# Second MLP: the weight sum for product N7 is tied to a place behind the remainder of the unit ahead

## The chip, the cores and the metric

The kernel runs on one core of one Trainium2 chip. The metric is device time in microseconds, from launch to end. Three runs of the kernel before gave 2282.0, 2282.33 and 2283.88 us, median 2282.33. The execution that was profiled took 2283.91 us itself, and its span from the first to the last instruction was 2282.1 us, so 1.81 us lie around the span.

## The reference

256 tokens of width 2048 go through one attention layer (MLA), a squared-ReLU MLP, one Mamba-2 layer and a second squared-ReLU MLP, all with RMS norm before and a residual sum behind. Only the second MLP is touched here. It is

```
h = rms_norm(x, mlp_norm_g[1])        # 256 x 2048
u = relu(h @ w_in)                    # w_in  2048 x 8192
x = x + (u * u) @ w_out               # w_out 8192 x 2048
```

in float32.

## The kernel before

**Exact products from halves.** A weight tile arrives in float32. ScalarE copies it to a rounded type (the high half, tile `wh`, L102), VectorE subtracts this from the original (the remainder, tile `wl`, L103), and TensorE forms three products: high by high (L619), high of the activations by remainder of the weights (L620), remainder of the activations by high (L621). So each weight tile of 128 x 1024 costs one ScalarE and one VectorE instruction before TensorE may read it. Such a tile is a *unit*. Units are numbered through the program and stand in one list; `wh819` and `wl819` are the two halves of unit 819. There are four buffers each for `wh` and `wl`, so the halves of unit 819 reuse those of unit 815 once TensorE is through with them. Six raw buffers hold tiles that come from memory, on SyncE's queue, in the order of the list.

**Seven products instead of eight.** The first matrix product of the MLP, with `w_in`, goes pair of column blocks by pair of column blocks: `p` counts the pairs, 0 to 7. Pair 0 is done plainly. For pairs 1 to 7, called passes here, the 2x2 blocks (two halves of the tokens, two halves of the input rows, two column blocks) are combined in the manner of Strassen, and the seven products have names: M1, N7, N5, N6, N4, M2, N3. Each comes in four units, `d` = 0 to 3, called quarters of the rows here. The weights of a quarter are b11, b12, b21 and b22. M1 takes b11 as it is. N7 needs b12 + b22, which VectorE adds in the place of b22 (L183). N5 then needs b11 + b12, added in the place of b12. N6 needs b11 + b12 + b22, added in the place of b11. M2, N3 and N4 need no sum on VectorE; N4's is made by a DMA of GpSimd that adds b21 onto the tile that N6 used. So N7's sum reads two tiles fresh from memory, while the other two sums read tiles that are there by then.

**The order of the list.** `plan()` interleaves the units of a pass with those of the second matrix product (`o`, with `w_out`, of the hidden blocks of earlier passes), by a table of costs. Units of a pass take 6 matmuls on TensorE, `o` units and the plain `c` units 12. Stretches of the list in the second MLP that are spoken of below:

| units | what they are |
|---|---|
| 695 to 702 | pass 1: M1, N7, N5, N6 of quarter 2; M1, N7, N5 of quarter 3; N4 of quarter 1 |
| 816, 817, 819, 820 | pass 4, quarter 0: M1, N7, N5, N6 (818 and 821 are `o` units) |
| 822, 823 | pass 4, quarter 1: M1, N7 |
| 829, 830, 831, 832, 833, 834 | pass 4: N6 of quarter 1; M1, N7 of quarter 2; an `o` unit, the last of its block; N5, N6 of quarter 2 |

**Who sets the order of the instructions.** TensorE's order is the order in which the program is written. On the other engines a scheduler sets it when the program is built, from its own estimates of when each instruction could run; each engine then takes its instructions strictly in that order, and one that waits holds back all behind it. `issue_after(ins)` is a tie: what is written under it may not stand ahead of `ins` on the engine of `ins`. `flow.last_lo` is the latest remainder that was written (the last L103), which is the one of the unit ahead in the list. The kernel before uses this tie for N7's sum in the Mamba-2 layer (`prefix == ("s",)`), not in the two MLPs (`prefix == ("s", 0)` and `("s", 1)`).

**Other work on the two engines.** VectorE also adds finished `o` blocks onto the residual (L438, two instructions, one for each half of the tokens), combines finished products (L623, L624) and makes remainders of hidden activations (L301). ScalarE also copies M1's finished product out of its bank (L633), applies ReLU and square (L579, L627, L569) and makes high halves of activations (L300).

Of the kernel before, what the change touches and what calls it, by code (L numbers as in the profile page):

```python
# [71 lines left out]
class Flow:  # L72
# [22 lines left out]
    def halves(self, raw, n, step=None):  # L95

        nc = self.nc
        h = self.pools["wh"].tile([P, 1024], F32R, tag="wh", name=f"wh{self.done}")
        lo = self.pools["wl"].tile([P, 1024], F32R, tag="wl", name=f"wl{self.done}")
        for o in range(0, n, step or n):  # L100
            v = slice(o, o + (step or n))
            self.last = nc.scalar.activation(h[:, v], raw[:, v], AF.Copy)  # L102
            self.last_lo = nc.vector.tensor_tensor(lo[:, v], raw[:, v], h[:, v].bitcast(F32), ALU.subtract)  # L103
        return h, lo
# [65 lines left out]
def seven(prefix, p, src):  # L170

    state = {}

    def quarter(d, i, j):
        return src[2 * i + d // 2, 2 * p + j][:, (d % 2) * 1024:(d % 2) * 1024 + 1024]

    def unit(flow, name, d):  # L180
        nc = flow.nc
        st = state.setdefault(d, {})
        add = lambda out, a, b: nc.vector.tensor_tensor(st[out].tile, st[a].tile, st[b].tile, ALU.add)  # L183
        halves = lambda q: flow.halves(st[q].tile, 1024)

        def make():
            if name == "N7":
                with flow.tc.issue_after(flow.last_lo.ins) if prefix == ("s",) else nullcontext():
                    add("b22", "b12", "b22")
                out = halves("b22")  # L190
                if d in LATE5:
                    nc.gpsimd.dma_start(st["b12"].tile, quarter(d, 0, 0), accum_op=ALU.add)
                return out
            if name == "N5" and d not in LATE5:
                add("b12", "b11", "b12")
                return halves("b12")
            if name == "N6":
                add("b11", "b11", "b22")
                out = halves("b11")
                nc.gpsimd.dma_start(st["b11"].tile, quarter(d, 1, 0), accum_op=ALU.add)  # L200
                return out
            return halves({"M1": "b11", "N4": "b11", "N5": "b12"}.get(name, name))

        def load(k, pool, q):
            st[k] = Load(pool, quarter(d, *q))
            return st[k]

        loads = {"M1": lambda: [load("b11", "rx", (0, 0))],
                 "N7": lambda: [load("b12", B12, (0, 1)), load("b22", "raw", (1, 1))],
                 "M2": lambda: [load("M2", "raw", (1, 0))], "N3": lambda: [load("N3", "raw", (1, 1))]}  # L210
        return Unit(prefix + (p, name, d), 2, 512, loads.get(name, list)(), make)

    return unit
# [1596 lines left out]
```

## Time and profile before

| what | us |
|---|---|
| profiled execution, own time | 2283.91 |
| its span | 2282.1 |
| TensorE busy in the span | 2269.3 (99%) |
| VectorE busy | 1965.0 (86%) |
| ScalarE busy | 1442.3 (63%) |
| second MLP, 1590 to 2282 us of the span | 692 |
| TensorE busy in it | 686.54 |
| VectorE busy in it | 604.76 |
| ScalarE busy in it | 422.84 |

The page of the profile lists for each engine its busy time, for each line of the program the time of its instructions, and for each wait the engine that ended it. TensorE is the engine that is nearly always busy. Its matmuls are pipelined: one of 512 columns is shown with some 0.39 us, but the next starts 0.23 us after it. So lost time on TensorE is best read from the starts of matmuls that follow each other: what goes beyond 0.23 us was lost. In rows of the timeline, the first number is the start in us from the start of the span, the second the duration; behind them stand engine, line, operation, tiles (out<-in) and count, and in brackets the idle time ahead of it and what ended it.

### The profile page before, as it was taken

To read this page: it belongs to the slowest core of one execution; us is meant where nothing else is said; L and a number is where in the kernel's file an instruction comes from. 1 tells how busy PE (TensorE), PEld (TensorE's weight loads), DVE (VectorE), ACT (ScalarE), POOL (GpSimd) and SP (SyncE) were. 2 spreads that over 40 slices of the span, in tenths; PEclk is the share of its full clock that TensorE was granted. 3 is DMA by queue.
4 is the path that set the end of the run, shared out by engine and by line. 5 is a ranking of instruction groups with operands and counts; after the bars stand their busy time and mean duration, and the time that the engine had idled before them with its cause. 6 is when DMAs were issued, how large, how long until landed. Compare 5 with 4: busy or idle time off the path is not lost.

```text
span 2282.1 us, 30858 instructions
## 1 busy us (share of the span) xinstructions
PE 2269.3 (99%) x10881; PEld 1880.4 (82%) x10881; DVE 1965.0 (86%) x2257; ACT 1442.3 (63%) x2044; POOL 284.9 (12%) x339
## 2 busy tenths in 40 slices
PE   9999999999999999999999999999999999999999
PEld 7898888888888888888888788888888888888887
DVE  7786697998998897879979998976989889989985
ACT  6775475666666666566677676565666665665663
POOL 1440000000000000100003532230000000000000
PEclk9999999999999999999999999999999999999999
DMA  8545778888888877768898888866788888888874
GB/s 316 173 153 156 214 229 263 261 258 267 264 254 259 270 236 245 237 190 272 262 368 284 290 290 310 295 220 218 215 256 253 254 270 251 262 275 238 264 233 162
DMA packets 176026, 569.74 MB, mean 250 GB/s; under 512 B 20192, under 2 KB 29344, under 8 KB 175872
## 3 DMA queue, kind: packets, MB, share of 16 engines
q1 hardware_dynamic: 147808, 498.24, 65.2%
q0 software_dynamic: 16320, 56.88, 11.9%
q10 hardware_dynamic: 11744, 12.66, 1.8%
q8 instruction: 85, 1.39, 0.2%
q14 instruction: 69, 0.57, 0.1%
HBM read 542.23 MB, written 6.41 MB: 240 GB/s over the span
## 4 chain that ended last, share of the span: by engine, by line
PE 93%; DVE 3%; DMA 2%; ACT 1%; issue 1%; POOL 0%; SPq 0%; ACTq 0%; DVEq 0%
PE acc L340 10%; PE acc L341 10%; PE acc L344 10%; PE yp L621 9%; PE yp L620 9%; PE yp L619 9%; PE st L620 7%; PE st L621 7%; PE st L619 7%; DVE wl L103 1%; DMA wraw<-mi 1%; PE st L1164 1%; PE st L1162 1%; PE st L1163 1%; PE yp L340 1%; PE yp L341 1%
## 5 line engine op out<-in xcount | busy, mean ns | idle before, releaser
L102 ACT ACTIVATE wh<-wraw 128x1024 fp32r<-128x1024 f32 (+1 forms) x818 | 857.3, 1053 | 531.2 <-PE acc L341 179.8
L103 DVE TENSOR_TENSOR wl<-wraw,wh 128x1024 fp32r<-128x1024 f32 (+1 forms) x818 | 988.2, 1227 | 179.0 <-ACT wh L102 168.9
L619 PE MATMUL yp<-wh,k 128*128 128x512 f32 x896 | 349.3, 390 | 0.0
L621 PE MATMUL yp<-wh,k 128*128 128x512 f32 x896 | 348.8, 389 | 0.0
L620 PE MATMUL yp<-wl,k 128*128 128x512 f32 x896 | 348.6, 389 | 0.0
L102 ACT ACTIVATE wh<-wrx 128x1024 fp32r<-128x1024 f32 x192 | 203.2, 1059 | 168.7 <-PE yp L621 99.6
L103 DVE TENSOR_TENSOR wl<-wrx,wh 128x1024 fp32r<-128x1024 f32 x192 | 233.6, 1222 | 41.0 <-ACT wh L102 39.5
L340 PE MATMUL acc<-wh,k 128*128 128x512 f32 x496 | 196.9, 397 | 0.3 <-ACT k L300 0.3
L621 PEld LDWEIGHTS yp<-wh,k 128*128 128x128 f32 x896 | 168.2, 188 | 35.1
L619 PEld LDWEIGHTS yp<-wh,k 128*128 128x128 f32 x896 | 168.3, 188 | 34.8
L620 PEld LDWEIGHTS yp<-wl,k 128*128 128x128 f32 x896 | 168.2, 188 | 34.8
L341 PE MATMUL acc<-wh,k 128*128 128x512 f32 x496 | 193.7, 391 | 0.6 <-DVE k L301 0.6
L340 PE MATMUL acc<-wh,xt 128*128 128x512 f32 x480 | 191.6, 399 | 0.9 <-ACT wh L102 0.9
L341 PE MATMUL acc<-wh,xt 128*128 128x512 f32 x480 | 187.4, 390 | 0.2 <-DVE xt L484 0.2
L619 PE MATMUL st<-wh,xt 128*128 128x512 f32 x448 | 177.7, 397 | 0.0
L621 PE MATMUL st<-wh,xt 128*128 128x512 f32 x448 | 174.9, 390 | 0.0
L620 PE MATMUL st<-wl,xt 128*128 128x512 f32 x448 | 174.7, 390 | 0.0
L200 POOL DMA_DIRECT2D wrx<-mi x56 | 49.0, 875 | 723.8 <-DVE wl L103 513.0
L620 PE MATMUL st<-wl,sN 128*128 128x512 f32 x336 | 131.5, 391 | 2.9 <-DVE wl L103 2.9
L619 PE MATMUL st<-wh,sN 128*128 128x512 f32 x336 | 133.3, 397 | 0.1
L344 PE MATMUL acc<-wl,k 128*128 128x512 f32 x496 | 132.7, 389 | 0.0
L621 PE MATMUL st<-wh,sN 128*128 128x512 f32 x336 | 131.1, 390 | 0.0
(342 smaller groups left out, 3808.2 us busy)
## 6 DMA issues: line engine op xcount, KB each, us to landing
wraw<-mi SPq DMA_DIRECT2D x256, 512.0 KB, 5.7
wraw<-mo SPq DMA_DIRECT2D x256, 512.0 KB, 5.3
wraw<-si SPq DMA_DIRECT2D x160, 512.0 KB, 6.1
wraw<-so SPq DMA_DIRECT2D x64, 512.0 KB, 5.1
wrx<-mi SPq DMA_DIRECT2D x56, 512.0 KB, 5.4
wrx<-mi POOLq DMA_DIRECT2D x56, 512.0 KB, 7.7
wraw<-wo SPq DMA_DIRECT2D x32, 512.0 KB, 3.8
tap<-xD SPq DMA_DIRECT2D x24, 512.0 KB, 8.2
```

What stands on the lines that cost most here:

```text
L102: self.last = nc.scalar.activation(h[:, v], raw[:, v], AF.Copy)
L103: self.last_lo = nc.vector.tensor_tensor(lo[:, v], raw[:, v], h[:, v].bitcast(F32), ALU.subtract)
L200: nc.gpsimd.dma_start(st["b11"].tile, quarter(d, 1, 0), accum_op=ALU.add)
L340: nc.tensor.matmul(accs[t][:, :n], ah, wh[:, q, :], start=first and kt + q == 0, stop=False)
L341: nc.tensor.matmul(accs[t][:, :n], al, wh[:, q, :], start=False, stop=False)
L344: nc.tensor.matmul(accs[t][:, :n], lhs(kt + q, t)[0], wl[:, q, :], start=False, stop=en and q == nk - 1)
L619: nc.tensor.matmul(b, ah, wh, start=first and q == 0, stop=False)
L620: nc.tensor.matmul(b, ah, wl, start=False, stop=False)
L621: nc.tensor.matmul(b, al, wh, start=False, stop=last and q == 1)
L1162: nc.tensor.matmul(bank[onto], ah, wh, start=done + q == 0 and not skip, stop=False, skip_group_check=skip)
L1163: nc.tensor.matmul(bank[onto], al, wh, start=False, stop=False, skip_group_check=skip)
L1164: nc.tensor.matmul(bank[onto], ah, wl, start=False, stop=done == 3 and q == 1, skip_group_check=skip)
```

## The change

In the second MLP, N7's sum (L183 under `if name == "N7"`) is now tied behind the latest remainder, in all passes and quarters but pass 1, quarter 0: 27 of its 28 sums. The first MLP stays as it was, and the Mamba-2 layer too.

```
-                with flow.tc.issue_after(flow.last_lo.ins) if prefix == ("s",) else nullcontext():
+                with flow.tc.issue_after(flow.last_lo.ins) if prefix == ("s",) or prefix == ("s", 1) and (p, d) != (1, 0) else nullcontext():
                     add("b22", "b12", "b22")
```

No instruction is added or taken away. The orders of TensorE, GpSimd and SyncE's queue are the same; VectorE's and ScalarE's differ from the second MLP's pass 1 on. Three places:

VectorE in pass 4, quarters 0 and 1 (`wl819`, `wl820`: remainders of N5 and N6 of quarter 0; `wraw823_17479`: the sum for N7 of quarter 1; `wrx816`: the sum for N6 of quarter 0):

```order
-L183 TENSOR_TENSOR wraw823_17479<-wraw823_17477,wraw823_17479 128x1024
+L183 TENSOR_TENSOR wrx816_17365<-wrx816_17365,wraw817_17379 128x1024
 L301 TENSOR_TENSOR k4_1173_17317<-sm_1181_17455,k4_1172_17316 128x4x128
 L103 TENSOR_TENSOR wl819_17467<-wraw817_17377,wh819_17466 128x1024
-L183 TENSOR_TENSOR wrx816_17365<-wrx816_17365,wraw817_17379 128x1024
-L183 TENSOR_TENSOR wraw823_17477<-wrx822_17463,wraw823_17477 128x1024
 L103 TENSOR_TENSOR wl820_17483<-wrx816_17365,wh820_17482 128x1024
 L103 TENSOR_TENSOR wl821_17496<-wraw821_17437,wh821_17495 128x1024
+L103 TENSOR_TENSOR wl822_17522<-wrx822_17463,wh822_17521 128x1024
```

The sum for unit 823 stood ahead of the remainder of unit 819; it now stands behind that of unit 822. The sum for N6 of quarter 0 now stands ahead of the remainder of unit 819.

VectorE in pass 4, quarter 2 (`wl833`, `wl834`: remainders of N5 and N6; `x00`, `x10`: the two residual sums of the `o` block that ends with unit 832):

```order
 L103 TENSOR_TENSOR wl833_17689<-wraw831_17611,wh833_17688 128x1024
+L183 TENSOR_TENSOR wrx830_17593<-wrx830_17593,wraw831_17613 128x1024
+L438 TENSOR_TENSOR x00_142<-yp_1188_17591,x00_142 128x512
+L438 TENSOR_TENSOR x10_146<-yp_1189_17592,x10_146 128x512
 L103 TENSOR_TENSOR wl834_17702<-wrx830_17593,wh834_17701 128x1024
 L103 TENSOR_TENSOR wl835_17713<-wraw835_17673,wh835_17712 128x1024
-L438 TENSOR_TENSOR x00_142<-yp_1188_17591,x00_142 128x512
-L438 TENSOR_TENSOR x10_146<-yp_1189_17592,x10_146 128x512
```

The two residual sums stood behind the remainder of unit 835; they now stand ahead of that of unit 834. The same move is there in passes 3, 5 and 6. In pass 2 only the first of the two moves ahead of that remainder; in pass 7 neither does.

ScalarE in pass 1, quarter 3 (`wh700`, `wh701`: high halves of N7 and N5; the L633 row copies M1's finished product):

```order
 L102 ACTIVATE wh699_15509<-wrx699_15451 128x1024
 L300 ACTIVATE k4_1089_15488<-sm_1094_15519 128x4x128
+L633 ACTIVATE s2_1095_15564<-st_1082_15250 128x512
 L102 ACTIVATE wh700_15529<-wraw700_15466 128x1024
+L300 ACTIVATE k4_1089_15488<-sm_1096_15566 128x4x128
 L102 ACTIVATE wh701_15542<-wraw700_15464 128x1024
 L102 ACTIVATE wh702_15554<-wrx687_15274 128x1024
-L633 ACTIVATE s2_1095_15564<-st_1082_15250 128x512
-L300 ACTIVATE k4_1089_15488<-sm_1096_15566 128x4x128
```

The copy of M1's product stood behind the high half of unit 702; it now stands ahead of that of unit 700. Unit 699 is the last of M1's four.

## The prediction

> **What bounds the kernel now.** I read the page's chain first, then the second MLP by itself in three views: busy time, what ended TensorE's idle time, what ended VectorE's.
>
> ```profile
> PE 93%; DVE 3%; DMA 2%; ACT 1%; issue 1%; POOL 0%; SPq 0%; ACTq 0%; DVEq 0%
> ```
>
> ```profile
> 1590.00:2282.00 692.00, 686.54 (x3121) 566.65 (x3119) 604.76 (x599) 422.84 (x461) 38.85 (x55) 1.00 0.80 244
> ...
> PE st L620 <- DVE wl L103: 2.3, 3, 0.8
> ...
> DVE wraw L183 <- DMA wraw<-mi: 13.1, 13, 1.6
> ```
>
> TensorE bounds it: 686.54 of 692.00 us busy, at a granted clock of 1.00, and 93% of the chain. The other 5.46 us are all that an edit of order can win. The waits view names one kind of stall: three times the matmul with the remainder waits for L103, 2.3 us together. VectorE, busy for 604.76 us, is the closest behind: it has 87 us free, so a late remainder is a matter of order, not of load. And 13 times it stands in L183 for a DMA, 13.1 us: a sum that stands so early in the order that its tile has not arrived, with all later remainders behind it. That is the instruction the change moves.
>
> **What is removed.** In pass 4 the stall looks like this, TensorE first, then VectorE and ScalarE.
>
> ```profile
> 1899.51 0.40 PE L621 MATMUL st<-wh,sN 128*128 128x512 f32 x1
> 1899.81 0.49 PE L619 MATMUL st<-wh,sN 128*128 128x512 f32 x1
> 1901.07 0.50 PE L620 MATMUL st<-wl,sN 128*128 128x512 f32 x1 [0.77 <-DVE wl L103]
> 1901.41 0.39 PE L621 MATMUL st<-wh,sN 128*128 128x512 f32 x1
> 1901.64 0.39 PE L619 MATMUL st<-wh,sN 128*128 128x512 f32 x1
> ```
>
> ```profile
> 1883.32 3.49 DVE L103 TENSOR_TENSOR wl<-wraw,wh 128x1024 fp32r<-128x1024 f32 x3
> ...
> 1894.51 1.23 DVE L183 TENSOR_TENSOR wraw<-wraw,wraw 128x1024 f32<-128x1024 f32 x1 [1.40 <-DMA wraw<-mi]
> 1895.65 0.69 DVE L301 TENSOR_TENSOR k<-sm,k 128x512 fp32r<-128x512 f32 x1
> 1896.25 1.22 DVE L103 TENSOR_TENSOR wl<-wraw,wh 128x1024 fp32r<-128x1024 f32 x1
> 1897.38 1.22 DVE L183 TENSOR_TENSOR wrx<-wrx,wraw 128x1024 f32<-128x1024 f32 x1
> ...
> 1899.79 1.23 DVE L103 TENSOR_TENSOR wl<-wrx,wh 128x1024 fp32r<-128x1024 f32 x1
> ```
>
> ```profile
> 1898.69 1.07 ACT L102 ACTIVATE wh<-wrx 128x1024 fp32r<-128x1024 f32 x1 [4.44 <-DVE wrx L183]
> ```
>
> The sum of unit 823 waits 1.40 for its tile and takes 1.23; only then comes N6's sum (1897.38 to 1898.60), then ScalarE's high half (1898.69), then the remainder (1899.79 to 1901.02), then the matmul at 1901.07. TensorE's normal step between starts is 0.23 (1901.41 to 1901.64). Lost: 0.30 − 0.23 = 0.07 at 1899.81, 1.26 − 0.23 = 1.03 at 1901.07, and 0.34 − 0.23 = 0.11 behind it, where the pipeline fills again: 1.21 us.
>
> After the change, N6's sum stands six instructions of 1024 columns and one of 512 behind the three remainders that end at 1886.81. An instruction of the first kind holds VectorE for 1.14 (1894.51 to 1895.65), a short one for 0.60 (1895.65 to 1896.25). So the sum ends by 1886.81 + 6 × 1.14 + 0.60 = 1894.25, or some 0.6 later if ScalarE holds up one of the remainders; the high half and remainder of unit 820 are then through by about 1897.5, 2.4 ahead of their use. The stall is gone. The same place in passes 3, 5 and 6:
>
> ```profile
> 1815.47 0.44 PE L619 MATMUL st<-wh,sN 128*128 128x512 f32 x1
> 1816.67 0.50 PE L620 MATMUL st<-wl,sN 128*128 128x512 f32 x1 [0.76 <-DVE wl L103]
> 1817.01 0.39 PE L621 MATMUL st<-wh,sN 128*128 128x512 f32 x1
> ...
> 1984.15 0.40 PE L619 MATMUL st<-wh,sN 128*128 128x512 f32 x1
> 1984.42 0.50 PE L620 MATMUL st<-wl,sN 128*128 128x512 f32 x1
> 1984.75 0.40 PE L621 MATMUL st<-wh,sN 128*128 128x512 f32 x1
> ...
> 2067.27 0.40 PE L621 MATMUL st<-wh,sN 128*128 128x512 f32 x1
> 2067.76 0.50 PE L619 MATMUL st<-wh,sN 128*128 128x512 f32 x1
> 2069.02 0.50 PE L620 MATMUL st<-wl,sN 128*128 128x512 f32 x1 [0.76 <-DVE wl L103]
> 2069.36 0.39 PE L621 MATMUL st<-wh,sN 128*128 128x512 f32 x1
> ```
>
> Pass 3: 0.97 + 0.11 = 1.08. Pass 5: 0.04 + 0.10 = 0.14. Pass 6: 0.26 + 1.03 + 0.11 = 1.40. Together −(1.08 + 1.21 + 0.14 + 1.40) = **−3.83 us**. Bounds: −3.83, since I find no other stall that the moved sum causes, and about half, −1.9, if a remainder ahead comes late.
>
> **What the new order adds: pass 1, quarter 3.** ScalarE's copy of M1's product (L633) now stands ahead of the high halves of units 700 and 701. It cannot start before TensorE ends M1's last unit, which it waits for in the bracket below; the two TensorE rows are the first matmuls that read the remainders of units 700 and 701.
>
> ```profile
> 1667.39 0.40 PE L620 MATMUL st<-wl,sN 128*128 128x512 f32 x1
> ...
> 1668.77 0.39 PE L620 MATMUL st<-wl,sN 128*128 128x512 f32 x1
> ```
>
> ```profile
> 1663.66 2.00 ACT L102 ACTIVATE wh<-wraw 128x1024 fp32r<-128x1024 f32 x2
> ...
> 1666.92 0.60 ACT L633 ACTIVATE s<-st 128x512 f32<-128x512 f32 x1 [0.30 <-PE st L621]
> 1667.42 0.59 ACT L300 ACTIVATE k<-sm 128x512 fp32r<-128x512 f32 x1
> ```
>
> Before, the two high halves ran from 1663.66 to 1665.66, and ScalarE then waited until 1666.92 for the copy. Now the copy goes first, at 1666.92 as before, and unit 700's high half takes the place at 1667.42, where the split of activations (L300) stood: to 1668.48. The remainder follows to 1669.73 (1.22 us), and the matmul due at 1667.39 starts at 1669.78: 2.39 late, with 0.11 for the refill 2.50. Next the high part of the moved split ends at 1668.97, unit 701's high half runs to 1669.93, the low part of the split on VectorE from 1669.64 to 1670.24, unit 701's remainder to 1671.46. Its matmul, due at 1668.77 + 2.50 = 1671.27, starts at 1671.51: 0.24 and 0.11 more. Sum **+2.85 us**. No cover hides it, since the queue behind the copy is what TensorE reads next. Bounds: +2.39, and +3.99 if VectorE is one more instruction (1.14) behind.
>
> **What it adds: quarter 2 of passes 3 to 6.** The two residual sums (L438) now stand ahead of the remainder of unit 834. The second needs the last matmul of unit 832.
>
> ```profile
> 1927.44 0.39 PE L620 MATMUL st<-wl,sN 128*128 128x512 f32 x1
> ```
>
> ```profile
> 1926.06 1.06 ACT L102 ACTIVATE wh<-wraw 128x1024 fp32r<-128x1024 f32 x1 [1.65 <-PE yp L621]
> ```
>
> ```profile
> 1923.12 1.23 DVE L103 TENSOR_TENSOR wl<-wrx,wh 128x1024 fp32r<-128x1024 f32 x1 [0.15 <-ACT wh L102]
> ...
> 1925.58 1.28 DVE L438 TENSOR_TENSOR x<-yp,x 128x512 f32<-128x512 f32 x2
> ```
>
> The end of that matmul reaches the other engines at 1926.06, as ScalarE's row shows, which waits for the same yp product. The remainder of unit 834, done at 1924.35 before, now waits for the second residual sum: 1926.06 + 0.60 = 1926.66, plus 1.22 = 1927.88, so the matmul due at 1927.44 starts at about 1927.93: 0.49 late, 0.11 refill, 0.60 in all. Four passes: **+2.4 us**. In pass 2 only the first of the two sums is ahead, so 0.60 of this falls away and the remainder is 0.1 early; pass 7 keeps the old order there. Bounds: 0 (a hand-off half a microsecond faster than the row) and 4 × 1.2 = +4.8 (one more short instruction of 0.60 in the way). I take 2.4, from the row of the very release.
>
> **What costs nothing.** The 27 moved sums take 1.22 as before. The DMA waits of the sums go where the sum is moved behind the arrival; where they stay, only remainders used 2 us later stand behind them. The raw buffers come free up to 2 us later in a few places, with loads then issued several us ahead of their use; no instruction or DMA is added, and SyncE's queue keeps its order.
>
> **The sum**: −3.83 + 2.85 + 2.4 = +1.4 us. The profiled execution took 2283.91 (2282.1 span, 1.81 around it), so the like of it would take 2285.3. It lies 1.58 above the median of the runs; on the median 2282.33 + 1.4 = **2283.7**.
>
> **Rivals.**
>
> *Only the removal acts (faster).* If the two additions cost nothing: 2282.33 − 3.83 = 2278.5. For it: 87 us free on VectorE, and the residual sums are late by only 0.49. Against: L633's release at 1666.92 is a fact of TensorE's order, so 2.39 stays unless ScalarE's queue differs. Decides: whether the matmul at 1667.39 waits.
>
> *The sums come too late (slower).* In quarter 2 the moved sum for N7 and its companion for N5 stand together directly between M1's remainder and N7's, so N7's high half starts only after the sum, in line with its use.
>
> ```profile
> 1915.24 1.06 ACT L102 ACTIVATE wh<-wrx 128x1024 fp32r<-128x1024 f32 x1 [0.31 <-PE st L621]
> ```
>
> ```profile
> 1914.80 1.23 DVE L183 TENSOR_TENSOR wraw<-wrx,wraw 128x1024 f32<-128x1024 f32 x1
> 1915.94 2.35 DVE L103 TENSOR_TENSOR wl<-wrx,wh 128x1024 fp32r<-128x1024 f32 x2
> ```
>
> ```profile
> 1922.01 0.39 PE L620 MATMUL st<-wl,sN 128*128 128x512 f32 x1
> ```
>
> With the sum of 1914.80 moved behind it, M1's remainder can follow its high half (1915.24 + 1.06 = 1916.30) and end at about 1917.55. The sum, the high half and the remainder in a row (1.14 + 1.06 + 1.22 and hand-offs of 0.03) then end at about 1921.0, against a need at 1922.01: 1.0 of spare. From a lateness of 1.0 on it decides; a lateness of 1.9 (one more 1024-column instruction and a hand-off) costs 0.9 in each of six passes, +5.4: 2283.7 + 5.4 = 2289.1. Against it: VectorE's order there puts nothing else between.
>
> *The clock falls.* The new wait of 2.39 is three times the longest in the second MLP (0.77); the trace cannot show what the granted clock does after one. At the start of the kernel it shows cold matmuls:
>
> ```profile
> 1.44 4.21 PE L454 MATMUL warmed<-warm 128*128 128x512 f32 x9 [1.44 <-DVE warm L451]
> ```
>
> Nine in 4.21 us, against 8 × 0.23 + 0.39 = 2.23 at the normal step: one such stretch costs 2.0, so 2283.7 + 2.0 = 2285.7. The Trainium skill, "TensorE: Matmul & The Clock Gate", section "Part 1: The HAM clock gate (the "warmup" mystery)", says that TensorE falls to half rate only after an idle window of about 3.4 us; by that rule a wait of 2.39 leaves the clock alone, and no run here shows a wait of that length yet.
>
> *The change moves nothing that TensorE feels*: 2282.3; it would need the removal and the additions to be off by the same amounts.
>
> **How the numbers follow.** The sum as worked out 0.71, only the removal 0.12, late sums 0.09, clock 0.03, nothing 0.05. The likeliest case's own range, by its bounds (all low: −3.83 + 2.39 + 0; high: −1.9 + 2.85 + 2.4, or −3.83 + 3.99 + 4.8), is 2280.9 to 2287.3. From the fast rival to just short of the slow one the range is 2278.4 to 2286.8. What a measurement can tell from no change is about 0.2%, 4.6 us: faster means below 2277.8, past the full removal, 0.03; slower means above 2286.9, the late-sums case and a little of the high end, 0.10; the same 0.87.
>
> **What would show it.** After the change: no stall on the remainder of N6, quarter 0, in passes 3 to 6, and few of L183's waits for a DMA; a new wait of about 1.9 idle on TensorE in pass 1 near 1667 with L633 ahead of it on ScalarE; four short new gaps of about 0.5 at N6 of quarter 2, ended by L103, with L438 right ahead. If gaps show at N7 of quarter 2 instead, the slow rival holds. If the second MLP is shorter by more than 3 us, my additions are wrong; longer by more than 5, something late is missing in my list.

## The result, and the profile after

| | before | after |
|---|---|---|
| median, us (14 runs each) | 2282.6 (2280.88 to 2288.94) | 2286.61 (2285.17 to 2290.49) |
| ratio to before, 95% interval | | 1.0017 (1.0009 to 1.0024) |
| profiled execution, own time | 2283.91 | 2287.61 |
| its span | 2282.1 | 2285.8 |

The change costs 4.0 us, 0.17%: less than the 0.2% that count as a change here, but its interval, +2.1 to +5.5 us, does not hold 0. The forecast was 2283.7, +1.4 us.

Where the 3.70 us between the two profiled executions came from is read from TensorE's clock times at three places that are the same in both programs: the last matmul ahead of the second MLP, one behind pass 1, one at the end. Before:

```profile
1590.15 0.39 PE L341 MATMUL acc<-wh,k 128*128 128x512 f32 x1
...
1714.40 0.40 PE L620 MATMUL st<-wl,xt 128*128 128x512 f32 x1
...
2235.14 0.40 PE L341 MATMUL acc<-wh,k 128*128 128x512 f32 x1
```

After:

```profile
1590.41 0.39 PE L341 MATMUL acc<-wh,k 128*128 128x512 f32 x1
...
1719.59 0.39 PE L620 MATMUL st<-wl,xt 128*128 128x512 f32 x1
...
2238.84 0.40 PE L341 MATMUL acc<-wh,k 128*128 128x512 f32 x1
```

After is 0.26 late at the first, 5.19 at the second, 3.70 at the third. So pass 1 cost 4.93 us, where 2.85 was forecast, and passes 2 to 7 gave 1.49 back, where 3.83 − 2.4 = 1.43 was forecast.

**Passes 2 to 7** went as worked out. What ended TensorE's idle time in the second MLP, after:

```profile
PE st L620 <- DVE wl L103: 2.5, 6, 0.8
PE st L619 <- ACT wh L102: 1.2, 1, 1.2
```

VectorE's waits in L183 for a DMA, 13 of them before, do not appear in that view any more. At N6 of pass 4, quarter 0, VectorE and TensorE now read:

```profile
1898.03 1.22 DVE L183 TENSOR_TENSOR wrx<-wrx,wraw 128x1024 f32<-128x1024 f32 x1
...
1900.90 1.22 DVE L103 TENSOR_TENSOR wl<-wrx,wh 128x1024 fp32r<-128x1024 f32 x1
```

```profile
1904.42 0.39 PE L619 MATMUL st<-wh,sN 128*128 128x512 f32 x1
1904.64 0.39 PE L620 MATMUL st<-wl,sN 128*128 128x512 f32 x1
1904.87 0.39 PE L621 MATMUL st<-wh,sN 128*128 128x512 f32 x1
```

The remainder ends at 1902.12, 2.52 us ahead of the matmul at 1904.64 (2.4 was forecast), and the starts are 0.23 apart: the stall is gone. At N6 of quarter 2 the new wait is there, with the residual sums ahead of it:

```profile
1928.83 1.37 DVE L438 TENSOR_TENSOR x<-yp,x 128x512 f32<-128x512 f32 x2 [0.25 <-PE yp L621]
1930.12 1.22 DVE L103 TENSOR_TENSOR wl<-wrx,wh 128x1024 fp32r<-128x1024 f32 x1
```

```profile
1930.67 0.39 PE L619 MATMUL st<-wh,sN 128*128 128x512 f32 x1
1931.39 0.50 PE L620 MATMUL st<-wl,sN 128*128 128x512 f32 x1 [0.33 <-DVE wl L103]
1931.72 0.39 PE L621 MATMUL st<-wh,sN 128*128 128x512 f32 x1
```

0.72 − 0.23 = 0.49, and 0.33 − 0.23 = 0.10 behind it: the forecast's 0.49 and 0.11, in each of passes 3 to 6.

**Pass 1** did not. TensorE, after:

```profile
1664.28 0.40 PE L619 MATMUL st<-wh,sN 128*128 128x512 f32 x1
1665.12 0.50 PE L620 MATMUL st<-wl,sN 128*128 128x512 f32 x1 [0.45 <-DVE wl L103]
1665.46 0.40 PE L621 MATMUL st<-wh,sN 128*128 128x512 f32 x1
...
1667.78 0.60 PE L325 MATMUL sm<-ident,s 128*128 128x128 f32 x4
1669.57 0.50 PE L619 MATMUL st<-wh,sN 128*128 128x512 f32 x1 [1.20 <-ACT wh L102]
1670.83 0.50 PE L620 MATMUL st<-wl,sN 128*128 128x512 f32 x1 [0.76 <-DVE wl L103]
1671.17 0.45 PE L621 MATMUL st<-wh,sN 128*128 128x512 f32 x1
1671.42 0.63 PE L619 MATMUL st<-wh,sN 128*128 128x512 f32 x1
1671.85 0.63 PE L620 MATMUL st<-wl,sN 128*128 128x512 f32 x1
```

Three things are read from it. At 1665.12 there is a wait that the forecast did not have: 0.84 − 0.23 = 0.61, and 0.11 behind it, at unit 698 (N6 of quarter 2). At unit 700 the first matmul starts 1.79 behind the transposes (L325), against 0.36 before, and the second 1.26 behind the first, against 0.31: 1.43 + 0.95 = 2.38, where 2.39 was forecast, and 0.11 behind it. Before, the transposes and the first matmul stood so; the second, at 1667.39, stands in the prediction:

```profile
1666.72 0.60 PE L325 MATMUL sm<-ident,s 128*128 128x128 f32 x4
1667.08 0.48 PE L619 MATMUL st<-wh,sN 128*128 128x512 f32 x1
```

And from 1671.42 on the matmuls follow each other every 0.43 us instead of 0.23. The table of stretches of 2 us shows why; the number behind the busy times of the engines is the granted clock:

```profile
1670.00:1672.00 2.00, 1.24 (x5) 0.97 (x5) 2.00 (x3) 2.00 (x4) 0.00 (x0) 0.84 0.23 43
1672.00:1674.00 2.00, 2.00 (x7) 1.52 (x6) 2.00 (x3) 1.90 (x2) 0.00 (x0) 0.50 0.25 33
1674.00:1676.00 2.00, 2.00 (x9) 1.61 (x8) 1.91 (x2) 0.77 (x1) 0.00 (x0) 0.81 0.85 254
```

Behind the wait the clock fell to a half for some 3.4 us (the three rows lose 0.32 + 1.00 + 0.38 = 1.70 us of full clock). 0.72 + 2.49 + 1.7 = 4.9 us: the 4.93 of pass 1.

### The profile page after: what moved, and what is told of

The parts are those of the page before. It is cut to its first block, busy times and chain, and to the rows that moved or that the text cites. A ratio compares the mean times of both kernels' runs of the same rounds, so it can differ in the third digit from the quotient of the medians.

```text
span 2285.8 us, 30863 instructions
## 1 busy us (share of the span) xinstructions
PE 2272.8 (99%) x10881; PEld 1883.0 (82%) x10881; DVE 1968.0 (86%) x2257; ACT 1439.0 (63%) x2044; POOL 281.7 (12%) x339
## 4 chain that ended last, share of the span: by engine, by line
PE 96%; DVE 2%; ACT 1%; DMA 1%; issue 0%; POOL 0%; SPq 0%; ACTq 0%; DVEq 0%
PE acc L340 10%; PE acc L341 10%; PE acc L344 10%; PE yp L619 9%; PE yp L621 9%; PE yp L620 9%; PE st L620 8%; PE st L621 8%; PE st L619 8%; PE st L1162 1%; PE st L1164 1%; PE st L1163 1%; PE yp L340 1%; PE yp L341 1%; PE yp L344 1%; PE sm L325 1%
```

## The experiments

The changes against before are the ratio on record of this kernel's runs to the runs of before taken beside it, with its 95% interval, less 1 and times 2283 us. The ratio is not quite that of the two medians: for the change without pass 1 it gives −1.6 us where the medians differ by 1.0, for the copy put back +2.5 where they differ by 1.7. In the code, `...` stands for what is left out of a line.

**One quarter alone: the removal.** Only quarter 1 keeps the tie.

```
-  ... or prefix == ("s", 1) and (p, d) != (1, 0)
+  ... or prefix == ("s", 1) and d == 1 and p > 1
```

> Only the ties of quarter 1 in passes 2 to 7 are kept: the removal alone. Theory (the parts of the change add up): the four stalls at N6 of quarter 0 in passes 3 to 6 are gone, nothing is added in pass 1 and at N6 of quarter 2, -3.8 us against before, about 2278.8, and no matmul of the second MLP at half clock. Rival (removed stalls are given back later in the pass): within 1 us of before.

Measured: 0.9986 (0.9977 to 0.9995), −3.2 us (−5.3 to −1.1); medians 2280.28 and 2283.4. The view of TensorE's waits lists none in the second MLP, and the granted clock stays at 1.00. The removal is worth what its rows said, within the interval, and little of it is given back: by the starts of the matmuls in its profile the four places lose 3.80 us less than in that of before, and one place in pass 2, at 1761.44, loses 0.31 more.

**The change without pass 1.**

```
-  ... (p, d) != (1, 0)
+  ... p > 1
```

> The change without its ties in pass 1. Theory: removal -3.8 and the four waits behind the residual sums +2.4, so -1.4 us against before, some 5 us less than the change. Rival (what makes the change slower lies in passes 2 to 7): +2 to +4 us, as the change.

Measured: 0.9993 (0.9984 to 1.0001), −1.6 us (−3.7 to +0.2); medians 2282.42 and 2283.4. Its waits are the four at N6 of quarter 2, 1.3 us of idle time together, and nothing else:

```profile
PE st L620 <- DVE wl L103: 1.3, 4, 0.3
```

The rival, that passes 2 to 7 make the change slower, is out.

**Pass 1 alone.**

```
-  ... (p, d) != (1, 0)
+  ... p == 1 and d > 0
```

> Only the ties of pass 1, quarters 1 to 3. Theory: waits of 0.7 us at N6 of quarter 2 and 2.4 to 2.5 us at N7 of quarter 3 (+3.2 together), and behind them about 3.4 us of matmuls at half clock (+1.7): +4.9 us with the clock drop in nearly every execution. Rival (the clock drop was an accident of the one profiled execution): +3.2 us in the mean, and the granted clock of the executions as before.

Measured: 1.0018 (1.0009 to 1.0027), +4.1 us (+2.1 to +6.2); medians 2287.54 and 2283.4. The whole size of the change's loss is there with pass 1 alone. Its profile shows the same waits and the same fall of the clock to a half, over 7 matmuls. One of 11 executions had a mean granted clock of 1.000, the others 0.999 or 0.998; of the 33 of before, 17 had 1.000. (The clock can dip elsewhere too: the profile of the change has 0.91 between 1260 and 1280 us, in the Mamba-2 layer, which the edit does not touch, and before's has none there. Of the 14 profiled kernels 7 have this dip, so a mean of 0.999 does not by itself point to pass 1.)

**The change without quarter 2.** ScalarE's order is that of the change.

```
-  ... (p, d) != (1, 0)
+  ... (p, d) != (1, 0) and (p == 1 or d != 2)
```

> The change without the ties of quarter 2 in passes 2 to 7; ScalarE's order is that of the change. Theory: the four short waits at N6 of quarter 2 are gone, 2.4 us less than the change, so +1.6 us against before. Rival (those waits hide other idle time): as the change, +4 us.

Measured: 1.0004 (0.9995 to 1.0013), +0.9 us (−1.1 to +3.0); medians 2284.17 and 2283.4. The four waits are gone; that is 3.1 us less than the change's +4.0, and the intervals hold the 2.4 that the waits cost by their rows. Its profiled execution shows pass 1 without the fall of the clock:

```profile
1670.31 0.60 PE L325 MATMUL sm<-ident,s 128*128 128x128 f32 x4
1672.11 0.50 PE L619 MATMUL st<-wh,sN 128*128 128x512 f32 x1 [1.20 <-ACT wh L102]
1673.37 0.50 PE L620 MATMUL st<-wl,sN 128*128 128x512 f32 x1 [0.76 <-DVE wl L103]
...
1674.65 0.39 PE L619 MATMUL st<-wh,sN 128*128 128x512 f32 x1
1675.10 0.50 PE L620 MATMUL st<-wl,sN 128*128 128x512 f32 x1
1675.44 0.40 PE L621 MATMUL st<-wh,sN 128*128 128x512 f32 x1
```

The same waits to the hundredth, 1.20 and 0.76, and this time the clock stayed. What decides is shown below, behind the waits of chosen length. And at full clock the wait at unit 701 shows, 0.45 − 0.23 = 0.22 and 0.11 behind it, where 0.24 and 0.11 were forecast; in the profile of the change the slow matmuls cover it.

**Waits of chosen length: what drops the clock.** To the kernel with quarter 1 only, extra instructions are added behind N6's sum in quarter 0; they write the sum's own values back (the line is shortened).

```
                 add("b11", "b11", "b22")
+                [nc.vector.tensor_tensor(b11, b11, b11, ALU.max) for _ in range(N[p])]   # second MLP, d == 0
```

> Quarter 1 only, and in passes 2 to 7 the sum for N6 of quarter 0 is followed by 4, 5, 6, 5, 7 and 6 extra instructions of 1.14 us on VectorE (they write the sum's own values back), so that TensorE waits at that unit: by the spare time of the run with quarter 1 only (about 3.2 us) some 1.4, 2.5, 3.6, 2.5, 4.8 and 3.6 us, in two pieces, the last of 0.8 us. Theory (the clock drops when TensorE was idle for most of a stretch of some 3 us, and the phase decides for waits near that): no drop after 1.4, a drop after some of those of 2.5, and after all of 3.6 and 4.8; each drop lasts about 3.4 us and costs 1.7. Rival (an idle stretch of 3.4 us without a matmul is needed): a drop after 4.8 at most. Second rival (the drop in pass 1 had another cause than the wait): no drop at all.

> The same kernel as the one before it in this call, a second execution. Theory: the same, and for the waits of about 2.5 us a different answer may come from the same place, since the phase of the clock's window is not tied to the program. Rivals as there.

> As the dose kernel, with 3, 2, 3, 3 and 2 extra instructions in passes 2 to 6 and none in pass 7. By the larger doses (one more instruction made TensorE 1.26 us later, five made it 5.2 late) TensorE is to be late by about 2.6, 1.3, 2.6, 2.6 and 1.3 us there. Theory (the clock drops when TensorE was idle for most of some window, with the phase deciding near the edge; in pass 1 of the change 2.4 us of waiting dropped it in two profiled executions and not in a third): no drop after 1.3, some of those after 2.6. Rival (any wait of a microsecond can drop it): drops after 1.3 too. Second rival (the edge lies above 2.6, and in pass 1 the wait of 0.7 ahead of the long one is needed as well): no drop at all.

> The same kernel, a second execution. Theory: the same waits, and among those of 2.6 us the drops may fall on other passes than in the first. Rivals as there.

Measured: 2328.59 and 2327.4 us for the larger doses, 2296.85 and 2303.22 for the smaller, before 2283.87 and 2284.29 beside them. The larger doses made TensorE later than I had worked out, so all of them lay above the edge, and the second pair was needed to find it. In the table, "late" is what the unit's first matmul and its first remainder matmul lost beyond the normal step, together.

| where | late, us | clock fell |
|---|---|---|
| smaller doses, passes 3 and 6, both executions | 1.4 | 0 of 4 |
| pass 1, unit 700, with the copy put back (below) | 2.0 | 0 of 1 |
| smaller doses, passes 4 and 5, both executions, and pass 2 of the first | 2.2 to 2.4 | 3 of 5 |
| pass 1, unit 700, with 0.7 lost some 5 us ahead: the change, pass 1 alone, without quarter 2 | 2.4 | 2 of 3 |
| pass 2 of the second execution of the smaller doses, and all larger doses | 3.3 and more | 13 of 13 |

Two stretches of 10 us with the same wait at the same place, pass 4, in the two executions of the smaller doses; first the one, then the other:

```profile
1902.00:1912.00 10.00, 8.25 (x31) 6.13 (x31) 7.68 (x9) 5.56 (x7) 0.90 (x1) 0.83 0.51 133
```

```profile
1910.00:1920.00 10.00, 8.25 (x39) 5.98 (x37) 9.29 (x11) 6.22 (x8) 0.90 (x1) 1.00 0.55 137
```

Here the first theory held on when the clock falls, and the rivals fell: it takes more than a microsecond, and less than an unbroken 3.4 us. An idle stretch of 1.20 and one of 0.76 around a single matmul of 0.50 is enough in about half of the cases. The theory's length of a fall, 3.4 us each, did not hold: 10 of the 16 behind the doses were longer (last section).

What decides in such a case can be read from the traces that are there. The granted clock changes only on a grid of 3.41 us: in all 14 traces the times between two changes are whole multiples of 3.41 us (in the change 1256.11, 3.41, 406.19, 3.41 and 610.99), and the grid lies at another place in each execution. Cut along its own grid, each trace gives the share of a step in which TensorE was busy, and the clock of the next step:

| step, us | TensorE busy | clock in the next step |
|---|---|---|
| the change, pass 1, 1667.94 to 1671.35 | 1.46 (0.43) | 0.50 |
| pass 1 alone, 1668.32 to 1671.73 | 1.46 (0.43) | 0.50 |
| without quarter 2, pass 1, 1669.12 to 1672.53 | 2.21 (0.65) | 1.00 |
| smaller doses, first execution, pass 4, 1902.49 to 1905.90 | 1.66 (0.49) | 0.50 |
| smaller doses, second execution, pass 4, 1912.30 to 1915.72 | 2.35 (0.69) | 1.00 |

In the 14 traces, without the last 10 us of each, the clock fell 25 times, each time behind a step in which TensorE was busy for at most 0.53 of it; only three other steps at full clock, all near 1258 us, were as low (0.48 to 0.52) without a fall. So one and the same wait drops the clock where it lies within one step, and not where the grid cuts it in two. And the 1.4 us of lateness, with idle stretches of 0.24 and 0.76, leave TensorE busy for 0.71 of a step wherever it lies (an estimate from these rows).

**Pass 1, quarter 2 alone.**

```
-  ... (p, d) != (1, 0)
+  ... (p, d) == (1, 2)
```

> Only the tie of pass 1, quarter 2. Theory: the wait at N6 of quarter 2 near 1665 (0.6 us and the refill of 0.1, at its second remainder matmul) comes from this tie alone, because the high half of N5 now stands behind a ReLU (L579) on ScalarE and behind its later sum: +0.7 us there, no wait at N7 of quarter 3. Rival (it takes the tie of quarter 3 too): no wait at N6 of quarter 2.

Measured: 2287.23 us in one execution, before 2283.87. The test does not tell the two apart. With quarter 3 not tied, its sum goes ahead of quarter 2's and waits 1.80 us for its tile; the waits that follow, at N7 and N5 of quarter 2, come to 2.1 us, and N6 has none: the rival's words, but by a cause that neither had. It shows that the tied quarters are not independent, and leaves the cause of the wait at unit 698 to the trace of the change: N5's high half waits for N5's sum, and unit 698's stands behind four instructions on hidden blocks:

```profile
1659.61 1.06 ACT L102 ACTIVATE wh<-wraw 128x1024 fp32r<-128x1024 f32 x1 [0.19 <-DVE wraw L183]
1660.58 1.25 ACT L579 ACTIVATE s<-yp,rs 128x512 f32<-128x512 f32 x2
1661.72 1.14 ACT L569 ACTIVATE s<-s 128x512 f32<-128x512 f32 x2
1662.76 2.00 ACT L102 ACTIVATE wh<-wrx 128x1024 fp32r<-128x1024 f32 x2
```

Before, unit 697's high half ran at 1656.90 and unit 698's at 1660.77: unit 698's is 2.0 us later now, and its remainder had 0.7 us to spare (it ended at 1663.53 and was used at 1664.21).

```profile
1656.90 1.06 ACT L102 ACTIVATE wh<-wraw 128x1024 fp32r<-128x1024 f32 x1 [0.25 <-PE st L621]
...
1660.77 1.05 ACT L102 ACTIVATE wh<-wrx 128x1024 fp32r<-128x1024 f32 x1
```

**Is it M1's copy, or the sum itself?** The prediction put the wait at unit 700 on the copy (L633) at the head of ScalarE's queue. In the profile of the change the sum of unit 700 ends at the moment at which the copy starts:

```profile
1666.72 1.22 DVE L183 TENSOR_TENSOR wraw<-wraw,wraw 128x1024 f32<-128x1024 f32 x1
```

```profile
1667.97 0.60 ACT L633 ACTIVATE s<-st 128x512 f32<-128x512 f32 x1 [2.73 <-PE st L621]
1668.47 1.05 ACT L102 ACTIVATE wh<-wraw 128x1024 fp32r<-128x1024 f32 x1
```

So two kernels tell them apart. The first is the change with the copy put back behind unit 702's high half:

```
-                nc.scalar.activation(v["m1"], bank["M1"], AF.Copy)
+                with self.tc.issue_after(self.flow.last.ins) if layer == 1 and p == 1 else nullcontext():
+                    nc.scalar.activation(v["m1"], bank["M1"], AF.Copy)
```

> The change, with the copy of M1's product (L633) in pass 1 tied behind the high half of unit 702, where it stood before; nothing else moves on any engine. First theory (the prediction's: the copy at the head of ScalarE's queue makes unit 700 late): the wait of 2.4 us at unit 700 is gone, and with it the clock drop; about +0.5 us against before instead of +4. Second theory (the moved sum itself is late: in the profile of the change it ends at 1667.94, as the copy starts, so unit 700's high half could not start before): the high half starts 0.5 earlier and no more, TensorE is still some 1.9 to 2.0 us late at unit 700, +3 to +3.5 us against before, the clock drops in part of the executions.

Measured: 1.0011 (1.0002 to 1.0020), +2.5 us (+0.5 to +4.6); medians 2285.36 and 2283.7. ScalarE now waits at the high half, and for the sum:

```profile
1670.20 1.06 ACT L102 ACTIVATE wh<-wraw 128x1024 fp32r<-128x1024 f32 x1 [2.73 <-DVE wraw L183]
```

```profile
1669.99 0.60 PE L325 MATMUL sm<-ident,s 128*128 128x128 f32 x4
1671.32 0.49 PE L619 MATMUL st<-wh,sN 128*128 128x512 f32 x1 [0.72 <-ACT wh L102]
1672.62 0.50 PE L620 MATMUL st<-wl,sN 128*128 128x512 f32 x1 [0.81 <-DVE wl L103]
```

(1.33 − 0.36) + (1.30 − 0.31) = 1.96 us late, 0.4 less than in the change: the second theory. The clock held here in this profile, and 6 of 11 executions had a mean granted clock of 1.000, against 4 of 14 of the change. By the steps of 3.41 us there is a reason: its two idle stretches, 0.72 + 0.81 = 1.53 us, leave TensorE busy for more than half of any step, where the change's 1.96 need not; this is an estimate from the rows. Fewer falls may be what the rest of the gain is, but it is not shown: the kernel without quarter 2, with the change's waits in pass 1, had 6 of 11 too, and the intervals of +2.5 and +4.0 overlap. The time does not decide between the theories either (the interval begins at the first one's +0.5); the rows do.

The second ties quarter 3 of pass 1 only, so that unit 698 is in time and the copy stands behind unit 700's high half.

```
-  ... (p, d) != (1, 0)
+  ... (p, d) == (1, 3)
```

> Only the tie of pass 1, quarter 3. On ScalarE the high half of unit 700 now stands ahead of M1's copy, on VectorE the sum stands behind the split of the activations (L301) as in the change. First theory (the copy is the cause): no wait at unit 700's first matmul, and about 1 us at unit 701, whose high half stands behind the copy. Second theory (the late sum is): the sum ends near 1666.4, the high half near 1667.5, so waits of 0.4 us at unit 700's first matmul and 0.9 at its remainder, and about 0.8 at unit 701; no wait at N6 of quarter 2 (near 1664).

Measured: 2285.31 us in one execution, before 2283.7. No wait near 1664, and then

```profile
1665.98 0.60 PE L325 MATMUL sm<-ident,s 128*128 128x128 f32 x4
1666.68 0.49 PE L619 MATMUL st<-wh,sN 128*128 128x512 f32 x1
1667.99 0.50 PE L620 MATMUL st<-wl,sN 128*128 128x512 f32 x1 [0.81 <-DVE wl L103]
...
1669.24 0.40 PE L619 MATMUL st<-wh,sN 128*128 128x512 f32 x1
1670.26 0.50 PE L620 MATMUL st<-wl,sN 128*128 128x512 f32 x1 [0.62 <-DVE wl L103]
```

0.34 at unit 700's first matmul, 1.00 at its remainder, 0.79 at unit 701's: the second theory's 0.4, 0.9 and 0.8. At unit 700 no copy is ahead, and the first theory had no wait there; at unit 701 both had one.

**A version that beats both.** Quarter 1 in both MLPs, since the first has two waits of the same kind (in the profile of before the matmul is 0.46 and 0.44 us late, and the one behind it 0.11).

```
-  ... prefix == ("s", 1) and (p, d) != (1, 0)
+  ... len(prefix) == 2 and d == 1 and (p > 1 or prefix == ("s", 0))
```

> The ties of quarter 1 in both MLPs (in the first MLP passes 1 to 7). Theory: as with quarter 1 of the second MLP alone, -3.1 us by its runs, and the two waits of 0.57 and 0.44 us (with 0.11 behind one of them) at N6 of quarter 0 in the first MLP are gone: -1.1 more, -4.2 in all. Rival (ScalarE's order, in which four splits of activations now stand behind a high half, brings a new wait in the first MLP): -3 us or less of a gain.

Measured: 0.9983 (0.9974 to 0.9992), −3.9 us (−5.9 to −1.8); medians 2280.15 and 2283.87. TensorE waits for no weight tile in either stretch of the seven products. Its interval lies below 1 and clear of the change's, though 0.17% is less than the 0.2% that count here; that it beats quarter 1 of the second MLP alone (−3.2) is not shown, the intervals overlap.

## Why the prediction was right, and where it was not

The time, 2286.61, lies at the upper end of the range (2278.4 to 2286.8), and the forecast of no change by the 0.2% holds. The mean of the forecast is 2.9 us too low, 0.3 of it because the median of before was 2282.33 then and is 2282.6 beside the change. That the time lies inside by 0.2 us is partly luck: the upper end was put just short of the rival of the late sums, which did not happen, and what filled the room are two things that the sum did not have, a wait of 0.72 us in pass 1 and the fall of the clock. By its steps:

- **What is removed**, −3.83: right for the execution that was profiled. −3.2 (−5.3 to −1.1) with that part alone, and the remainder is 2.52 us early where 2.4 was worked out. The size varies between executions: in the three profiled kernels that keep before's order in passes 2 to 7 (pass 1 alone, its quarter 2, its quarter 3) the four places lose 2.7, 3.1 and 3.4 us. Why was not tried.
- **Quarter 2 of passes 3 to 6**, +2.4: right. 0.49 and 0.10 in each of the four passes. Pass 2 and pass 7 have no wait, as said.
- **Pass 1, quarter 3**, +2.85: the size is right (2.38 + 0.11, and 0.22 + 0.11 where the clock holds), the cause only in part. The copy is what the high half of unit 700 waits for last, as worked out. But the step "No cover hides it, since the queue behind the copy is what TensorE reads next" took the sum of unit 700 to be there when the copy starts. It ends just then, and without the copy ahead it still makes unit 700 late by 1.96 of the 2.38; the copy adds 0.4. Two arrivals fell on one point in time, and the row of the one that was already in the trace hid the other.
- **What costs nothing**: wrong for pass 1, quarter 2. "where they stay, only remainders used 2 us later stand behind them" overlooked the path over ScalarE: the moved sums hold back N5's high half, and with it the ReLUs and unit 698's high half behind it. 0.72 us.
- **The rival on the clock** had a chance of 0.03, as a case by itself. It is no other case: it comes on top of the likeliest one, in two of three profiles with this wait, and costs 1.7 us. The price given (2.0) was near. What failed is the sentence of the rule set beside it. The Trainium skill, "TensorE: Matmul & The Clock Gate", section "Part 1: The HAM clock gate (the "warmup" mystery)", has the clock fall after an idle window of some 3.4 us. Here it fell after 1.20 and 0.76 us of idle time with a matmul between them, so the measurement decides against the reading that TensorE must be idle for the whole window. The half rate that this section of the Trainium skill gives, and some 3.4 us until full rate is back, agree with 0.50 in the row and with the 3.41 us that the slow stretch of the change lasted; behind the doses 10 of 16 slow stretches were longer.
- **Late sums in quarter 2 of passes 2 to 7** (the slow rival): did not happen; neither the profile of the change nor those of its parts have a wait at N7 there. **Only the removal** and **nothing moves** did not happen either.

With the two corrections the sum is −3.83 + 2.4 + 2.85 + 0.72, +2.1 without a fall of the clock; with one it is 1.7 more, less the 0.3 that the slow matmuls cover at unit 701: +3.5. The profiled executions differ by 3.70 − 0.26 = 3.44 in the second MLP, and the interval of the medians, +2.1 to +5.5, holds both sums.

## What to carry to other kernels

A tie that lets a sum stand later is worth having where the sum waits for its tile (quarter 1) and can cost where the sum is already in time (pass 1, and quarter 2 of passes 3 to 6); so it is to be set place by place, here by the one condition that gave −3.2 us instead of +4.0. When an instruction is moved, follow each of the engines that its result goes through, and list all arrivals at the point of use, not the last one that the old trace names. A wait on a TensorE that is otherwise always busy can have a second price: here waits that made it 2.2 to 2.4 us late dropped the clock in 5 of 8 cases, and the half-rate stretch behind one cost 1.7 us more in the change.

## What was not expected of the hardware

The clock falls behind less idle time than the prediction had: never at 1.4 us of lateness (4 cases), in 5 of 8 at 2.2 to 2.4, always from 3.3 (13 cases). The same wait at the same instruction dropped it in one execution and not in another, by where the grid of 3.41 us lay, so a single profile with a granted clock of 1.00 does not say that a wait is harmless. The slow stretches behind the doses, with matmuls 0.43 us apart, lasted one, two or three steps: 6 times 3.41, 9 times 6.83, once 10.24 us. In the 14 traces the clock stayed low behind a slow step in which TensorE was busy for at most 0.82 of it, and came back behind one with 0.85 or more. These shares are read from the traces as they are; no run was made to find the limits.
